# A decoder layer's opening regrouped: low parts off GpSimd, wider sums for the conditioning, four steps over K, PSUM tiles of two blocks

## The chip, the cores and the metric

The kernel runs on one core of one Trainium2 chip. The metric is the device time of one execution in microseconds, the median of the runs of one kernel. Inside a core, five engines run their own instruction queues in order and wait for each other by semaphores: TensorE (matrix products; the profile calls it PE, its weight loads PEld), VectorE (DVE), ScalarE (ACT), GpSimd (POOL) and SyncE (SP, which here only issues DMAs). Matrix products write to PSUM, eight banks of 512 f32 columns; all else lives in SBUF, 128 partitions wide.

## The reference

One decoder layer with adaLN conditioning, 256 tokens, width 2048, all f32, weights of some 630 MB read once:

```python
mods = silu(c) @ w_ada + b_ada                  # 9 vectors of 2048: shift, scale, gate, three times
sh1, sc1, g1, sh2, sc2, g2, sh3, sc3, g3 = split(mods, 9)
f1 = swiglu(x * (1 + sc1) + sh1, w_ffn1)        # 2048 -> 2 x 5632 -> 2048
x = layer_norm(alpha * x + 0.5 * g1 * f1)
m = hybrid_mixer(x * (1 + sc2) + sh2, ...)      # gated linear attention, dilated attention, output product
x = layer_norm(alpha * x + g2 * m)
f2 = swiglu(x * (1 + sc3) + sh3, w_ffn2)
x = layer_norm(alpha * x + 0.5 * g3 * f2)
```

The change concerns the start: the shift and scale of the first sub-layer are needed before any product of the first SwiGLU can be made, and they need 33.5 MB of `w_ada`.

## The kernel before

**The weight stream.** All large products run as one stream of *units*. A unit is two k-tiles (2 x 128 rows) of 512 columns of a weight, multiplied with both blocks of 128 tokens. Each f32 operand is split into two parts in a reduced format, `wh` (rounded) and `wl` (the rest), and a product is made of three matmuls (L239 to L241: high x high, high x low, low x high), so a unit is 12 matmuls. Weights come in loads of 1 MB (`raw`, an item, two units), three under way. ScalarE makes `wh` by a rounding copy (L223), VectorE or GpSimd makes `wl` by a subtraction of 128 x 1024 (L233). Who makes it is the flag `u.ve`: GpSimd for 38 units among the first 96 (units 0 and 1, then 3, 5, ... 29, then every third from 32 to 95) and for the first ones after each of the first two norms (`EARLY`, 12 units together), VectorE for all others.

**The order.** Instructions are emitted by one Python loop over units `p`, and each engine works off its queue in that order. For each `p` the loop splits unit `p + 3` (its `wh` and `wl`), emits the 12 matmuls of unit `p`, advances the side work by one step (`fl.step()`: transposes, modulation, the handling of finished sums, the norms), and then takes as many steps of the conditioning as a table `pace` of (unit, steps) demands by `p`.

**The conditioning.** `silu(c) @ w_ada` is summed on VectorE: one step (L388 the first, L390 the others) multiplies a k-tile of 512 columns by a value per partition and adds it to `part`; sixteen steps end a *piece*. Then TensorE transposes the four tiles of `part` (L424), VectorE reduces them (L341) and adds the bias (L346, L348). The first pieces, whose loads are called `abig`, hold shift and scale of the first sub-layer: two pieces with 256 columns of each, then three pairs of pieces with 512 columns of the scale and 512 of the shift. Eight pieces of 16 steps, 128 steps, precede the other seven vectors (loads called `araw`).

**The first chunks.** A *chunk* is 512 output columns. Since the modulated input becomes ready by columns, the first six gate and six up chunks are summed over K in five steps: `PHASES = ((0, 2), (2, 2), (4, 4), (8, 4), (12, 4))`, as (first k-tile, k-tiles). In steps 0 and 1 a chunk has one unit (units 0 to 11, 12 to 23), in the others two (24 to 47, 48 to 71, 72 to 95). After each step the sums leave PSUM: ScalarE copies them to `part8` after step 0, VectorE adds to it after steps 1 to 3 (L604, one 128 x 512 add for each token block), and after step 4 it adds them up and finishes the chunk (L610 to L616). `x1_groups` makes the modulated input for each group of columns (L432, L430, L410, L414).

**PSUM.** Four banks serve the sums (one tile for each token block, two chunks under way), four the transposes and other small things.

**The norms.** Behind each of the first two sub-layers, per token block: statistics (L446, L451), root and reciprocal (L458 to L460), normalising (L470), transposes, modulation, split (L408 to L432). The units of the next chunk are split during that.

```python
        while ns < min(len(units), p + 1 + SA + u.more):
            split(units[ns])
            ns += 1
        ...
        emit(u)
        fl.step()
        while ada["n"] < due(p):
            ada_step()
```

Of the kernel before, what the change touches and what calls it, by code (L numbers as in the profile page):

```python
# [35 lines left out]
# columns of the constants  # L36
# [27 lines left out]
EARLY = 10  # L64
# [7 lines left out]
class Flow:  # L72
    """Side work beside the weight stream: generators that yield where an engine has to wait for another."""
# [47 lines left out]
class Lhs:  # L121
    """An activation with features on partitions, in tiles of four k-tiles: two exact parts."""
# [12 lines left out]
class Item:  # L135
    """1 MB of a weight: G k-tiles of NC5 columns, or wide: H k-tiles of 2 * NC5"""
# [5 lines left out]
class Unit:  # L142
    def __init__(self, item, j, ts, chunk, first, last):
        self.item, self.j, self.ts, self.chunk, self.first, self.last = item, j, ts, chunk, first, last
        self.ve = self.more = 0
# [3 lines left out]
def layer(ctx, tc, a):  # L149
# [7 lines left out]
    pa = pool("pacc", 4, space=bass.MemoryType.PSUM)  # L157
# [19 lines left out]
    items, units, starts = [], [], {}  # L177

    class Chunk:
        """ps[t] = lhs[k0:k0+nk].T @ w[r0:r0+nk*P, c0:c0+512]; then done(t, ps[t])"""  # L180

        def __init__(self, w, r0, c0, nk, lhs, done, k0=0, head=False, tail=False, wide=None):
            self.lhs, self.done, self.k0, self.ps = lhs, done, k0, None
# [7 lines left out]
            seq, early = [], 0  # L191
            both = tuple(range(NT))
            n = len(its)
            gs = list(range(n))
            if head:
                seq += [(g, j, (t,)) for t in both for g in gs[:2] for j in range(2)]
                gs = gs[2:]
                early = EARLY
            mid = gs[:-2] if tail else gs
            seq += [(g, j, both) for g in mid for j in range(2)]  # L200
            if tail:
                seq += [(g, j, (t,)) for t in both for g in gs[-2:] for j in range(2)]
            for g, j, ts in seq:
                u = Unit(its[g], j, ts, self, g == 0 and j == 0, g == n - 1 and j == 1)
                u.k = k0 + g * G + j * H
                u.ve = early > 0
                early -= 1
                if early == EARLY - 1 and len(units):
                    units[-1].more = 1
                units.append(u)  # L210
# [32 lines left out]
    def emit(u):  # L243
        c, it = u.chunk, u.item
        if c.ps is None:
            fl.until(lambda: n_acc.n >= NT)
            n_acc.n -= NT
            c.ps = [pa.tile([P, NC5], F32, tag="acc", name="acc") for _ in range(NT)]
        wh, wl = it.wh[u.j]
        lhs = {(i, t): c.lhs.get(u.k + i, t) for t in u.ts for i in range(H)}  # L250
        for t in u.ts:
            for i in range(H):
                xh, xl = lhs[i, t]
                mm3(c.ps[t], xh, xl, wh[:, i], wl[:, i], u.first and i == 0, u.last and i == H - 1)
        if u.last:
            for t in u.ts:
                fl.spawn(c.done(t, c.ps[t]))

# [52 lines left out]
    def ada_load():  # L311
# [6 lines left out]
        if i < BIG:  # L318
            t = blk([P, n, NC5], name="abig")
        else:  # L320
            t = st.tile([P, n, NC5], F32, tag="araw", name="araw", bufs=3)
# [3 lines left out]
        else:  # L325
            for j in range(2):
                nc.sync.dma_start(t[:, :, j * 256:(j + 1) * 256],
                                  w[:, j * D + k0 * P:j * D + k0 * P + 256].rearrange("(k p) n -> p k n", p=P))
# [3 lines left out]
    def ada_reduce(ms, k0, nk, part, wait):  # L332
        if wait:
            yield wait
        if ms[0] in modc:
            ps = yield from mps([P, 4, P])
            transpose4(ps, part, 0)
            if ms[0] > 1:
                yield
            tot = tp.tile([P, 4], F32, tag="tot", name="tot")  # L340
            V.tensor_reduce(tot, ps, axis=mybir.AxisListType.X, op=ALU.add)  # L341
            for i, m in enumerate(ms):
                b = bcol(m)[:, k0:k0 + nk]
                o = modc[m][:, k0:k0 + nk]
                if m in PLUS1:
                    V.scalar_tensor_tensor(o, tot[:, i * nk:(i + 1) * nk], 1.0, b, op0=ALU.add, op1=ALU.add)  # L346
                else:
                    V.tensor_add(o, tot[:, i * nk:(i + 1) * nk], b)  # L348
# [19 lines left out]
    def ada_run():  # L368
        def prep(i):
# [3 lines left out]
            part = sp.tile([P, NC5], F32, tag="part", name="part", bufs=2)  # L373
# [66 lines left out]
    class Norm:  # L440
# [13 lines left out]
        def rstd(self, mv):  # L454
            """1 / sqrt(var + eps), -mean / sqrt(var + eps)"""
# [7 lines left out]
        def apply(self, t, mv, rs, nm):  # L463
            """y -> (y - mean) * rstd"""
# [9 lines left out]
    def ln_to(i, X, scm, shm, after):  # L474
        """per token block: the normalised rows, then the modulated transpose into X; then x = n * g + b"""
# [67 lines left out]
    def sqrt_ready():  # L543
        """a first square root, for its table to be there when the norm comes"""
# [22 lines left out]
    def ffn(w_gu, w_dn, X, gm, ln, norm, parts, pieced):  # L567
# [26 lines left out]
        def pieced_sink(c, e, q, sg, hT, kg):  # L594
            def done(t, ps):
                if q == 0 and (c, e, t) == (c, 0, 0):
                    partial[c] = blk([P, 2, NT, NC5], name="part8")
                p = partial[c][:, e, t]
                if q == 0:
                    A_.copy(p, ps)  # L600
                    n_acc.give()
                    return
                if q < len(PHASES) - 1:
                    V.tensor_add(p, p, ps)  # L604
                    n_acc.give()
                    return
# [11 lines left out]
            return done  # L618
# [51 lines left out]
        for pi, part in enumerate(parts):  # L670
            hT = Lhs(fl)
            if pi == 0 and pieced:
                sgs = {c: [None, None] for c in part}
                for q, (k0, nk) in enumerate(PHASES):
                    if nk == 2:
                        for c in part[::2]:
                            for e in range(2):
                                it = Item(w_gu, k0 * P, e * DFF + c * NC5, True)
                                items.append(it)
                                for i in range(2):  # L680
                                    Chunk(w_gu, 0, 0, 2, X, pieced_sink(c + i, e, q, sgs[c + i], hT, c + i),
                                          k0=k0, wide=(it, i))
                    else:
                        for c in part:
                            for e in range(2):
                                Chunk(w_gu, k0 * P, e * DFF + c * NC5, nk, X,
                                      pieced_sink(c, e, q, sgs[c], hT, c), k0=k0)
# [9 lines left out]
    # ==== sub-layer 1 ====  # L697
# [52 lines left out]
    for u in units[:2] + units[3:30:2] + units[32:96:3]:  # L750
        u.ve = 1

    # ==== sub-layer 2 ====
# [7 lines left out]
    # rope tables  # L761
# [115 lines left out]
    def tok_T(src, t, ready, dst):  # L877
        """[tok, 512] in PSUM -> dst(kpair, t, psum [P, 2, P]), features on partitions"""
# [68 lines left out]
    def head_task(h):  # L947
# [14 lines left out]
        # (output columns, partitions, keys, queries)  # L962
# [107 lines left out]
    # -- dilated attention: one softmax over the three groups' keys --  # L1070
# [130 lines left out]
    # -- gated branch b, merge --  # L1201
# [60 lines left out]
    # ==== sub-layer 3 ====  # L1262
# [9 lines left out]
    def ln3(norm, t):  # L1272
# [22 lines left out]
        for q in LN3_GP[t]:  # L1295
# [45 lines left out]
    for p, u in enumerate(units):  # L1341
        while ns < min(len(units), p + 1 + SA + u.more):
            split(units[ns])
            ns += 1
        if p in (12, 28, 50):
            fl.until(lambda: n_sml.n >= NT)
            n_sml.n -= NT
            x_load((12, 28, 50).index(p) + 1)
# [31 lines left out]
```

## Time and profile before

| | |
|---|---|
| median of 3 runs | 2754.81 us (2753.57 to 2754.82) |
| profiled execution, first to last instruction | 2753.9 us |
| TensorE busy | 2662.9 us, 97% |
| VectorE busy | 1955.0 us, 71% |
| ScalarE busy | 1201.0 us, 44% |
| GpSimd busy | 170.9 us, 6% |
| read from HBM | 645.90 MB |
| chain that ended last | TensorE 86%, VectorE 10%, issue 2% |

Engines' busy times are sums over the whole span; what bounds a stage is read from that stage alone. The profiled execution is one run; its span is 0.9 us under the median of the runs.

### The profile page before, as it was taken

The page shows a single profiled execution, that of the slowest core. Times are in us where ns is not written, and L with a number is a line of the kernel's source. Part 1 is how long each engine was busy: PE and PEld are TensorE (multiplying, and loading weights), DVE is VectorE, ACT ScalarE, POOL GpSimd, SP SyncE. Part 2 cuts the span into 40 slices and gives each one's busy share as a digit, 9 for nine tenths or more (in the row PEclk, how much of TensorE's full clock was granted, in tenths as well). Part 3 has the DMA queues.
Part 4 walks back from the last instruction along what each step waited for, and adds up shares of the span by engine and source line. Part 5 has one row for each costly group of instructions (what it writes and reads, how often), then busy time and mean ns, then how long its engine had stood idle before and what let it go on. Part 6 is the DMA issues. An engine that isn't in the chain of part 4 may idle for free.

```text
span 2753.9 us, 31250 instructions
## 1 busy us (share of the span) xinstructions
PE 2662.9 (97%) x12043; PEld 2191.7 (80%) x12043; DVE 1955.0 (71%) x2386; ACT 1201.0 (44%) x1387; POOL 170.9 (6%) x121
## 2 busy tenths in 40 slices
PE   6899999999999999999999999999999999999997
PEld 4677778888887788888888888888778888888886
DVE  7999987877766787676666676667775755655556
ACT  4233444444344654444443444554354444443443
POOL 3322200000001000000000000000110000000001
PEclk9999999999999999999999999999999999999999
DMA  9777688888874676667657767667557667656653
GB/s 341 270 266 271 223 307 306 303 291 283 282 240 165 210 271 226 214 229 238 227 186 259 247 231 242 209 223 267 196 186 258 229 225 235 230 187 210 207 191 122
DMA packets 327045, 654.24 MB, mean 238 GB/s; under 512 B 13128, under 2 KB 21552, under 8 KB 325616
## 3 DMA queue, kind: packets, MB, share of 16 engines
q1 hardware_dynamic: 322352, 633.46, 67.7%
q0 software_dynamic: 4544, 18.79, 2.1%
q8 instruction: 94, 1.54, 0.2%
q14 instruction: 55, 0.45, 0.0%
HBM read 645.90 MB, written 6.29 MB: 237 GB/s over the span
## 4 chain that ended last, share of the span: by engine, by line
PE 86%; DVE 10%; issue 2%; ACT 1%; DMA 1%; POOL 0%; SPq 0%; DVEq 0%; ACTq 0%
PE acc L239 27%; PE acc L241 27%; PE acc L240 27%; DVE part L390 3%; PE mps L424 2%; DVE wl L233 2%; DVE part L604 1%; DVE lhs L414 1%; PE mps L1163 1%; PE mps L1135 1%; ACT wh L223 0%; PE mps L973 0%; DVE sg L616 0%; DVE xm L432 0%; DMA abig<-in_w_ada 0%
## 5 line engine op out<-in xcount | busy, mean ns | idle before, releaser
L233 DVE TENSOR_TENSOR wl<-raw,wh 128x1024 fp32r<-128x1024 f32 x862 | 1066.1, 1239 | 696.2 <-ACT wh L223 694.8
L223 ACT CAST wh<-raw 128x1024 fp32r<-128x1024 f32 x912 | 957.4, 1053 | 1341.5 <-PE acc L241 1281.0
L239 PE MATMUL acc<-wh,lhs 128*128 128x512 f32 x3648 | 1445.8, 396 | 21.7 <-DVE part L604 9.7
L240 PE MATMUL acc<-wl,lhs 128*128 128x512 f32 x3648 | 1428.2, 392 | 5.7 <-DVE wl L233 4.4
L241 PE MATMUL acc<-wh,lhs 128*128 128x512 f32 x3648 | 1427.6, 391 | 0.6 <-DVE lhs L414 0.6
L239 PEld LDWEIGHTS acc<-wh,lhs 128*128 128x128 f32 x3648 | 689.5, 189 | 170.4 <-issue 8.9
L240 PEld LDWEIGHTS acc<-wl,lhs 128*128 128x128 f32 x3648 | 689.8, 189 | 152.6 <-DVE wl L233 8.1
L241 PEld LDWEIGHTS acc<-wh,lhs 128*128 128x128 f32 x3648 | 688.7, 189 | 147.7 <-DVE lhs L414 2.2
L390 DVE SCALAR_TENSOR_TENSOR part<-araw,cact,part 128x512 f32<-128x512 f32 x432 | 322.6, 747 | 0.5
L233 POOL TENSOR_TENSOR wl<-raw,wh 128x1024 fp32r<-128x1024 f32 x50 | 128.1, 2565 | 480.8 <-ACT wh L223 233.6
L390 DVE SCALAR_TENSOR_TENSOR part<-abig,cact,part 128x512 f32<-128x512 f32 x119 | 127.0, 1074 | 4.1 <-DMA abig<-in_w_ada 2.1
L604 DVE TENSOR_TENSOR part<-part,acc 128x512 f32<-128x512 f32 x72 | 46.1, 679 | 1.8 <-PE acc L241 1.8
L376 POOL DMA_DIRECT2D part<-in_b_ada x12 | 6.1, 506 | 627.3 <-DVE part L375 186.9
L414 DVE TENSOR_TENSOR lhs<-mps,lhs 128x512 fp32r<-128x512 f32 x64 | 41.3, 683 | 1.6 <-ACT lhs L410 1.6
L410 ACT CAST lhs<-mps 128x512 fp32r<-128x512 f32 x64 | 34.5, 586 | 0.0
L1064 POOL DMA_DIRECT2D mgd<-sga x8 | 4.3, 541 | 458.6 <-DVE sga L1062 457.8
L424 PE MATMUL mps<-ident,part 128*128 128x128 f32 x96 | 16.6, 300 | 15.6 <-DVE part L390 15.1
L414 DVE TENSOR_TENSOR lhs<-xm,lhs 128x256 fp32r<-128x256 f32 (+1 forms) x34 | 23.7, 714 | 10.3 <-ACT lhs L410 9.7
L424 PEld LDWEIGHTS mps<-ident,part 128*128 128x128 f32 x96 | 12.5, 153 | 20.4 <-DVE part L390 17.6
L1138 DVE TENSOR_TENSOR sS<-mps,consts 128x128 f32<-128x128 f32 (+1 forms) x48 | 16.0, 358 | 14.9 <-PE mps L1135 14.5
L612 ACT ACTIVATE sg<-sg 128x512 f32<-128x512 f32 x12 | 7.4, 633 | 43.9 <-DVE sg L610 43.9
L578 ACT ACTIVATE sg<-acc 128x512 f32<-128x512 f32 x32 | 19.0, 598 | 16.0 <-PE acc L241 16.0
(222 smaller groups left out, 942.2 us busy)
## 6 DMA issues: line engine op xcount, KB each, us to landing
raw<-in_w_ffn_gu SPq DMA_DIRECT2D x176, 1024.0 KB, 5.0
raw<-in_w_in SPq DMA_DIRECT2D x152, 1024.0 KB, 5.0
araw<-in_w_ada SPq DMA_DIRECT2D x224, 512.0 KB, 5.5
raw<-in_w_ffn_down SPq DMA_DIRECT2D x88, 1024.0 KB, 5.0
abig<-in_w_ada SPq DMA_DIRECT2D x24, 1024.0 KB, 7.9
raw<-in_w_branch_a SPq DMA_DIRECT2D x16, 1024.0 KB, 5.5
raw<-in_w_out SPq DMA_DIRECT2D x16, 1024.0 KB, 6.6
raw<-in_w_branch_b SPq DMA_DIRECT2D x8, 1024.0 KB, 4.9
```

What stands on the lines that cost most here:

```text
L223: A_.copy(wh, r)
L233: (nc.gpsimd if u.ve else V).tensor_sub(wl, r, wh.bitcast(F32))
L239: T.matmul(ps, lhsT=xh, rhs=wh, start=first, stop=False)
L240: T.matmul(ps, lhsT=xh, rhs=wl, start=False, stop=False)
L241: T.matmul(ps, lhsT=xl, rhs=wh, start=False, stop=last)
L390: V.scalar_tensor_tensor(pt, w, cact[:, k:k + 1], pt, op0=ALU.mult, op1=ALU.add)
L410: A_.copy(hs, src)
L414: V.tensor_sub(b[:, 1, j, t * P:(t + 1) * P], src, b[:, 0, j, t * P:(t + 1) * P].bitcast(F32))
L424: T.transpose(ps[:, j], src[:, c0 + j * P:c0 + (j + 1) * P], ident)
L604: V.tensor_add(p, p, ps)
L1135: T.matmul(ps[:, 0:nk], lhsT=qk[g][:, 0, j, t * P:(t + 1) * P], rhs=qk[g][:, 1, j, 0:nk], start=True, stop=True)
L1163: T.matmul(ops[:, 0:HD], lhsT=pTs[kb][:, g], rhs=d["v"][g][:, kb, j * HD:(j + 1) * HD], start=i == 0, stop=i == n_mm - 1)
```

## The change

Five edits belong together. No low part is made on GpSimd any more, neither in the opening nor after the norms, and the extra split ahead (`more`) goes. The conditioning's three pairs of pieces become three pieces of 1024 columns, scale and shift side by side, each step 128 x 1024; their 1 MB loads become two DMAs of half that size with half as many k-tiles, and `part` takes a buffer of the `araw` loads. The first vectors take 80 steps, not 128. The first chunks are summed in four steps of K, the last over eight k-tiles, four units a chunk (units 48 to 95). Both token blocks of a chunk share one PSUM tile of two banks, and after the first three steps one instruction handles both. The pace follows.

```diff
+SUMS = ((0, 2), (2, 2), (4, 4), (8, 8))
...
-        (nc.gpsimd if u.ve else V).tensor_sub(wl, r, wh.bitcast(F32))
+        V.tensor_sub(wl, r, wh.bitcast(F32))
...
-    pa = pool("pacc", 4, space=bass.MemoryType.PSUM)
+    pa = pool("pacc", 2, space=bass.MemoryType.PSUM)
...
-            c.ps = [pa.tile([P, NC5], F32, tag="acc", name="acc") for _ in range(NT)]
+            c.pair = pa.tile([P, NT, NC5], F32, tag="acc", name="acc")
+            c.ps = [c.pair[:, t] for t in range(NT)]
...
-        if u.last:
+        if u.last and c.both:
+            fl.spawn(c.done(c.pair))
+        elif u.last:
...
-        pieces += [((0, 1), k0, 2, 4 if k0 else 2)] if nk == 2 else [((1,), k0, 4, 4), ((0,), k0, 4, 4)]
+        pieces.append(((0, 1), k0, nk, 2 if nk == 4 or not k0 else 4))
...
-            t = blk([P, n, NC5], name="abig")
+            t = blk([P, n, len(ms) * nk * P], name="abig")
...
+            if len(pieces[i][0]) * pieces[i][2] == 8:
+                part = st.tile([P, 2 * NC5], F32, tag="araw", name="part", bufs=3)
...
+            def add(pair):
+                if (q, e) == (0, 0):
+                    partial[c] = blk([P, 2, NT, NC5], name="part8")
+                p = partial[c][:, e]
+                if q == 0:
+                    A_.copy(p, pair)
+                else:
+                    V.tensor_add(p, p, pair)
+                n_acc.give(NT)
...
-                for q, (k0, nk) in enumerate(PHASES):
+                for q, (k0, nk) in enumerate(SUMS):
...
-    for u in units[:2] + units[3:30:2] + units[32:96:3]:
-        u.ve = 1
...
-    pace = [(-1, 16), (5, 32), (20, 64), (42, 96), (66, 128), (n1 - 20, 320), (n1 + 8, 320), (n3 - 20, 512),
-            (n3 + 8, 512), (len(units) - 110, 576), (len(units) + 1, 576)]
+    pace = [(-1, 16), (5, 32), (20, 48), (33, 64), (45, 80), (n1 - 20, 272), (n1 + 8, 272), (n3 - 20, 464),
+            (n3 + 8, 464), (len(units) - 110, 528), (len(units) + 1, 528)]
...
-        while ns < min(len(units), p + 1 + SA + u.more):
+        while ns < min(len(units), p + 1 + SA):
...
-        if p in (12, 28, 50):
+        if p in (12, 24, 36):
```

## Rows read from the trace of the kernel before

**Rows 1.** The page's first line.
```profile
span 2753.9 us, 31250 instructions
```

**Rows 2.** Windows, all engines: stretch and length, busy us (instructions), clock, DMA share, GB/s.
```profile
24.50:51.60 27.10, 21.59 (x88) 17.26 (x87) 25.57 (x21) 16.43 (x23) 13.72 (x5) 0.97 1.06 404
51.60:121.30 69.70, 56.80 (x224) 44.39 (x224) 65.51 (x79) 22.67 (x31) 21.42 (x8) 0.89 0.78 281
121.30:198.90 77.60, 72.94 (x305) 58.30 (x305) 70.59 (x84) 30.81 (x37) 20.95 (x9) 0.93 0.74 267
...
276.90:356.20 79.30, 73.02 (x331) 57.76 (x330) 75.00 (x85) 32.23 (x43) 19.83 (x10) 1.00 0.70 239
356.20:800.00 443.80, 442.81 (x1990) 366.43 (x1990) 346.26 (x406) 190.29 (x202) 7.04 (x12) 1.00 0.86 294
```

**Rows 3.** Windows, L240 alone: PE busy (matmuls), PEld busy, clock, DMA share, GB/s.
```profile
0.00:121.30 121.30, 40.99 (x96) 20.29 (x96) 0.93 0.87 320
0.00:205.40 205.40, 83.27 (x200) 40.76 (x201) 0.93 0.80 292
0.00:276.90 276.90, 118.32 (x288) 57.84 (x289) 0.94 0.79 285
0.00:356.20 356.20, 156.20 (x384) 75.86 (x384) 0.95 0.77 275
356.20:800.00 443.80, 246.96 (x634) 119.19 (x635) 1.00 0.86 294
```

**Rows 4.** Chain of waits, 30 to 60 us: start, us, what.
```profile
33.96 2.78 DVE part L390
```

**Rows 5.** Timeline of GpSimd, 33 to 34 us: start, us, instruction, idle before.
```profile
33.67 2.51 POOL L233 TENSOR_TENSOR wl<-raw,wh 128x1024 fp32r<-128x1024 f32 x1 [3.40 <-ACT wh L223]
```

**Rows 6.** VectorE by line, 24.5 to 51.6 us: busy us, mean ns, idle before.
```profile
L390 DVE SCALAR_TENSOR_TENSOR part<-abig,cact,part 128x512 f32<-128x512 f32 x15 | 17.4, 1161 | 0.4
L233 DVE TENSOR_TENSOR wl<-raw,wh 128x1024 fp32r<-128x1024 f32 x4 | 6.2, 1554 | 0.9 <-ACT wh L223 0.9
L388 DVE TENSOR_SCALAR part<-abig,cact 128x512 f32<-128x512 f32 x1 | 2.4, 2412 | 0.1
```

**Rows 7.** VectorE by line, 51.6 to 124.1 us.
```profile
L390 DVE SCALAR_TENSOR_TENSOR part<-abig,cact,part 128x512 f32<-128x512 f32 x32 | 34.2, 1068 | 0.7
L233 DVE TENSOR_TENSOR wl<-raw,wh 128x1024 fp32r<-128x1024 f32 x8 | 14.1, 1768 | 0.0
L604 DVE TENSOR_TENSOR part<-part,acc 128x512 f32<-128x512 f32 x22 | 14.0, 679 | 0.0
```

**Rows 8.** VectorE by line, 124.1 to 198.9 us.
```profile
L390 DVE SCALAR_TENSOR_TENSOR part<-abig,cact,part 128x512 f32<-128x512 f32 x31 | 31.7, 1023 | 0.5
L233 DVE TENSOR_TENSOR wl<-raw,wh 128x1024 fp32r<-128x1024 f32 x15 | 20.4, 1363 | 0.0
L604 DVE TENSOR_TENSOR part<-part,acc 128x512 f32<-128x512 f32 x24 | 15.5, 679 | 1.8 <-PE acc L241 1.8
```

**Rows 9.** VectorE by line, 357 to 800 us.
```profile
L233 DVE TENSOR_TENSOR wl<-raw,wh 128x1024 fp32r<-128x1024 f32 x160 | 195.8, 1224 | 96.2 <-ACT wh L223 95.9
L390 DVE SCALAR_TENSOR_TENSOR part<-araw,cact,part 128x512 f32<-128x512 f32 x156 | 116.1, 744 | 0.3
```

**Rows 10.** Chain of waits, 822 to 845 us, the first norm.
```profile
823.48 1.94 DVE nm L460
825.43 5.06 DVE f L470 x2
```

**Rows 11.** Timeline of VectorE, 839 to 841 us, the same norm's second block.
```profile
839.91 0.16 DVE L460 SCALAR_TENSOR_TENSOR nm<-mv,rs 128x1 f32<-128x1 f32 x1
839.99 1.00 DVE L470 TENSOR_SCALAR f<-f,mv,rs 128x512 f32<-128x512 f32 x2
```

**Rows 12.** L233 on VectorE, 24 to 357 us: what it waited for (us, times).
```profile
  ACT wh L223: 4.6, 6
```

**Rows 13.** Timeline of VectorE, 822 to 860 us: three low parts in a row.
```profile
855.40 3.49 DVE L233 TENSOR_TENSOR wl<-raw,wh 128x1024 fp32r<-128x1024 f32 x3
```

More of the change, by code (lines that the diff above doesn't have):

```diff
@@ L59 @@
 PHASES = ((0, 2), (2, 2), (4, 4), (8, 4), (12, 4))
+SUMS = ((0, 2), (2, 2), (4, 4), (8, 8))
 ADA0 = 8
 ADA_FLIGHT = 3
-EARLY = 10
 LN_STEPS = ((3, 1, 1, 5), (2, 2, 0, 3))
@@ L144, in __init__ @@
         self.item, self.j, self.ts, self.chunk, self.first, self.last = item, j, ts, chunk, first, last
-        self.ve = self.more = 0
 @with_exitstack
@@ L179, in layer, with __init__ @@
     class Chunk:
-        def __init__(self, w, r0, c0, nk, lhs, done, k0=0, head=False, tail=False, wide=None):
-            self.lhs, self.done, self.k0, self.ps = lhs, done, k0, None
+        def __init__(self, w, r0, c0, nk, lhs, done, k0=0, head=False, tail=False, wide=None, both=False):
+            self.lhs, self.done, self.k0, self.ps, self.both = lhs, done, k0, None, both
             if wide:
@@ L190, in __init__ @@
             items.extend(its)
-            seq, early = [], 0
+            seq = []
             both = tuple(range(NT))
@@ L197, in __init__ @@
                 gs = gs[2:]
-                early = EARLY
             mid = gs[:-2] if tail else gs
@@ L205, in __init__ @@
                 u.k = k0 + g * G + j * H
[L206 to L209, printed above, removed]
                 units.append(u)
@@ L326, in ada_load @@
             for j in range(2):
-                nc.sync.dma_start(t[:, :, j * 256:(j + 1) * 256],
-                                  w[:, j * D + k0 * P:j * D + k0 * P + 256].rearrange("(k p) n -> p k n", p=P))
+                n2 = nk * P
+                nc.sync.dma_start(t[:, :, j * n2:(j + 1) * n2],
+                                  w[:, j * D + k0 * P:j * D + k0 * P + n2].rearrange("(k p) n -> p k n", p=P))
         ada["tiles"][i, g0] = t
@@ L335, in ada_reduce @@
         if ms[0] in modc:
-            ps = yield from mps([P, 4, P])
-            transpose4(ps, part, 0)
+            groups = [(ms, 0)] if len(ms) * nk == 4 else [((m,), i * NC5) for i, m in enumerate(ms)]
+            pss = []
+            for _, c0 in groups:
+                ps = yield from mps([P, 4, P])
+                transpose4(ps, part, c0)
+                pss.append(ps)
             if ms[0] > 1:
                 yield
[L340 to L348, printed above, removed]
+            for (gm, _), ps in zip(groups, pss):
+                tot = tp.tile([P, 4], F32, tag="tot", name="tot")
+                V.tensor_reduce(tot, ps, axis=mybir.AxisListType.X, op=ALU.add)
+                for i, m in enumerate(gm):
+                    b = bcol(m)[:, k0:k0 + nk]
+                    o = modc[m][:, k0:k0 + nk]
+                    if m in PLUS1:
+                        V.scalar_tensor_tensor(o, tot[:, i * nk:(i + 1) * nk], 1.0, b, op0=ALU.add, op1=ALU.add)
+                    else:
+                        V.tensor_add(o, tot[:, i * nk:(i + 1) * nk], b)
+            n_mps.give(len(groups) - 1)
         else:
@@ L372, in prep @@
             (m, *_), k0 = pieces[i][:2]
-            part = sp.tile([P, NC5], F32, tag="part", name="part", bufs=2)
+            if len(pieces[i][0]) * pieces[i][2] == 8:
+                part = st.tile([P, 2 * NC5], F32, tag="araw", name="part", bufs=3)
+            else:
+                part = sp.tile([P, NC5], F32, tag="part", name="part", bufs=2)
             if m not in modc:
@@ L594, in pieced_sink @@
         def pieced_sink(c, e, q, sg, hT, kg):
+            def add(pair):
[4 more added lines that the diff above has]
+                    A_.copy(p, pair)
+                else:
+                    V.tensor_add(p, p, pair)
+                n_acc.give(NT)
+                return
+                yield
             def done(t, ps):
-                if q == 0 and (c, e, t) == (c, 0, 0):
-                    partial[c] = blk([P, 2, NT, NC5], name="part8")
                 p = partial[c][:, e, t]
[L599 to L606, printed above, removed]
                 if e == 0:
@@ L617, in done @@
                     yield from up_tail(t, sg, hT, kg)
-            return done
+            return add if q < len(SUMS) - 1 else done
         def fold():
@@ L673, in ffn @@
                 sgs = {c: [None, None] for c in part}
-                for q, (k0, nk) in enumerate(PHASES):
+                for q, (k0, nk) in enumerate(SUMS):
+                    both = q < len(SUMS) - 1
                     if nk == 2:
@@ L681, in ffn @@
                                     Chunk(w_gu, 0, 0, 2, X, pieced_sink(c + i, e, q, sgs[c + i], hT, c + i),
-                                          k0=k0, wide=(it, i))
+                                          k0=k0, wide=(it, i), both=both)
                     else:
@@ L686, in ffn @@
                                 Chunk(w_gu, k0 * P, e * DFF + c * NC5, nk, X,
-                                      pieced_sink(c, e, q, sgs[c], hT, c), k0=k0)
+                                      pieced_sink(c, e, q, sgs[c], hT, c), k0=k0, both=both)
             else:
@@ L1341, in layer @@
     for p, u in enumerate(units):
-        while ns < min(len(units), p + 1 + SA + u.more):
+        while ns < min(len(units), p + 1 + SA):
             split(units[ns])
             ns += 1
-        if p in (12, 28, 50):
+        if p in (12, 24, 36):
             fl.until(lambda: n_sml.n >= NT)
             n_sml.n -= NT
-            x_load((12, 28, 50).index(p) + 1)
+            x_load((12, 24, 36).index(p) + 1)
         for gen in starts.get(p, ()):
```

## The prediction

> **What bounds the kernel now.** I read the windows by stage first, then the by-line tables of VectorE in the same stretches, then the chain of waits and the timeline in three short windows. The span is 2753.9 us [rows 1]; the median of the runs shown, 2754.81, is 0.9 us above it, which I add at the end. Four matmuls of L240 make one unit of the weight stream, so a count of them dates the units: unit 24 starts at 121.3 us, unit 50 at 205.4, unit 72 at 276.9, unit 96 at 356.2 [rows 3]. From 356.2 to 800 TensorE is 99.8% busy [rows 2] and passes 634 of these, 158.5 units, in 443.8 us: 2.80 us a unit with its side work [rows 3]. At that pace 96 units from 24.5 us on would end at 293; they end at 356.2, so the opening loses 63 us. In its stages shown VectorE is 91 to 95% busy, TensorE 80 to 94% [rows 2]: VectorE bounds the opening. From 356 to 800 it doesn't (78%). Of the rest only the two norms are touched, where the chain runs over VectorE too.
>
> **Where VectorE's time goes.** One step of the conditioning (L390) takes 0.744 us in a stretch without GpSimd low parts [rows 9]. The step at 33.96 takes 2.78 and ends 0.6 us after GpSimd's low part, which began at 33.67 and took 2.51 [rows 4, 5]. I read the excess as VectorE held up by GpSimd. By stage, taking off the means of 357 to 800 (0.744 for L390, 1.224 for L233): 24.5 to 51.6 has 15 x 0.417 + 4 x 0.330 + 1.7 for L388 (2.41 less a step) = 9.3 us [rows 6]; 51.6 to 124.1 has 32 x 0.324 + 8 x 0.544 = 14.7 [rows 7]; 124.1 to 198.9 has 31 x 0.279 + 15 x 0.139 = 10.7 [rows 8].
>
> **Prices.** A low part on VectorE: three in a row take 3.49 us, 1.16 each [rows 13]. A 1024-wide step isn't in the trace. A 512-wide add is 0.679 [rows 7], a 1024-wide difference 1.224 [rows 9], so another 512 columns cost 0.54, and 0.744 + 0.54 = 1.28 us. Bounds: 1.22 (that 1024-wide difference) and 1.49 (two narrow steps). I take 1.28, as both its terms are VectorE's own. A pair add: 0.679 + 0.54 = 1.22; bounds 1.36 (no better than two adds) and 1.08 (twice 0.54). I take 1.20.
>
> **The first 51.6 us.** Unit 0's low part now stands in VectorE's queue ahead of the first two modulated tiles: 1.16 us there against GpSimd's 2.5, both ahead of the second matmul; I count it as even. Then the second piece, not widened, sets the end: its 16th step releases the transposes that TensorE waits for. The stage loses 9.3 us of hold-ups and gains the low parts of units 1, 3, 5 and 7, 4 x 1.16 = 4.6. It ends 4.7 us earlier, at 46.9.
>
> **To unit 24.** Hold-ups -14.7; nine low parts (odd units 9 to 25) +10.4; 35 narrow steps (26.0) become 18 wide ones (23.0), -3.0; 11 pairs of adds, 11 x (1.36 - 1.20) = -1.8. Sum -9.1: unit 24 starts at 121.3 - 4.7 - 9.1 = 107.5, and all the features that it needs are there at 124.1 - 13.8 = 110.3.
>
> **Units 24 to 50.** Here the change costs. Before, the sums' fourth step took k-tiles 8 to 11 (from unit 48) and the fifth 12 to 15 (from unit 72); now the fourth takes 8 to 15, so unit 50 needs the last columns, and the new pace has the last wide step at unit 45 where the old one had the last narrow one at 66. From 110.3 VectorE must do 23 low parts (units 26 to 48), 26.7; 30 wide steps, 38.4; 13 pair adds, 15.6; and one group's reductions, modulation and waits, which is what is left of the same group before: 74.8 - 31.7 - 20.4 - 15.5 = 7.2 us [rows 8]. Sum 87.9: the last step ends at 198.2. TensorE then has eight transposes and units 47 to 49 to do, about 9.4 us, and VectorE brings the last columns in about that time; unit 50 starts at 207.6, 2 us later than before. All that is won to unit 24 is paid back here.
>
> **Units 50 to 96.** The gain shows here: the third add of the partial sums is gone, the wide steps are done, and nothing holds VectorE up. For eight units (a gate and an up chunk) VectorE has 8 x 1.16 = 9.3 of low parts, 8 x 0.946 x 0.744 = 5.6 of steps at the new pace, eight operations of some 0.68 to finish the chunks, 5.4, and 0.5 for gates: 20.8 us against TensorE's 22.4 at 2.80. So TensorE should bound. Its side work (two groups of four transposes in eight units) is denser here than from 356 to 800; I take 2.88 us a unit, near the lower of the bounds 2.80 and 3.30 (the last 24 units before, 79.3 us). 46 x 2.88 = 132.5, so unit 96 starts at 340.1 against 356.2: -16.1. From there both kernels have the same units. The pace is lighter on VectorE (192 steps over 203 units, not 182), but TensorE was at 99.8% there: worth nothing.
>
> **The two norms.** In the first, on the chain, a 128x1 product takes 1.94 us where its like takes 0.16, and two normalising steps 5.06 where two take 1.00 [rows 10, 11]: 5.8 us of hold-up by GpSimd low parts. These go to VectorE; by the order of the main loop one stands ahead of the reciprocal and one between the normalised rows and the modulation, 1.2 to 2.3 us on the path. Net -3.5 to -4.6; the later low parts and the lost extra split ahead are about even. I take -4 for each norm, -8. That the second is like the first is assumed from the same code.
>
> **At nothing.** Twelve pair copies on ScalarE replace 24: ScalarE is 33 to 61% busy in the opening [rows 2]; without that cover they'd cost some 12 x 1 us. The pair in PSUM frees both blocks at once where one could go first: a chunk two places on waits for it, at most half an add, 0.6 us, for each of 24 chunks, but VectorE's own queue is longer than that. Low parts wait in VectorE's queue for ScalarE's rounding copy, which GpSimd did on its own: those already on VectorE waited 4.6 us in 59 [rows 12], so 38 more might wait 3.
>
> **Sum.** 2753.9 - 16.1 - 8 + 0.9 = **2731 us**.
>
> **The queue of loads.** From 24.5 to 51.6 it is full and moves 404 GB/s; later 239 to 281, with 22 to 30% of its time free [rows 2]. Loads of 1 MB become two of half that, 24 more issues on SP's queue; the second piece's loads are split so already and lie in the 404 stretch, so I count nothing. The Trainium skill, "DMA: Bandwidth & Descriptors", section "Rules for kernel authors", speaks against this edit: it asks for 1 MiB or more in each DMA. By that rule the queue would be slower and rival (c) nearer; the 404 GB/s don't bear it out.
>
> **Rivals.**
> (a) VectorE still bounds to unit 96. Either the wide step costs 1.49, +0.21 x 46 = 9.7 us by unit 50, or TensorE keeps half of today's loss after it, (3.30 - 2.88) / 2 x 46 = 9.7. For it: 20.8 of 22.4 us is tight, in one in-order queue. Against it: the hold-ups that make today's loss are gone. 2741; with the norms' gain lost too, 2749.
> (b) The gain isn't there: the long rows are waits that come back under other names. If half of the 46 us (34.7 to unit 48, 11.6 in the norms) come back, the time is today's, 2755. Against it: 156 steps without GpSimd beside them have a mean of 0.744 [rows 9].
> (c) Slower: the queue of loads becomes the bound. Until unit 50 it must bring 33.6 MB of the conditioning (before 25.2), 26.2 of weights, 2 of x and some 3 ahead, 65 MB. At 404 GB/s that is 161 us, at 275, the mean from 0 to 356.2 [rows 3], 236: unit 50 would start 28 us late, the time 2759. It decides from 65 / (208 + 24) = 280 GB/s downwards. For it: after 51.6 no stage of the opening shows more than 281. Against it: they leave a quarter of the queue's time unused.
>
> **How the numbers follow.** Forecast 0.62 (its own range 2720 to 2738), (a) 0.20, (b) 0.07, (c) 0.08, and 0.03 that the time is under 2714, with VectorE no bound from early on. Two in ten lie outside from 2714 to 2747: (a) is inside but for its end, (b) and (c) are out. A change within 0.2%, 5.5 us, can hardly be told from none. Faster 0.85, same 0.07, slower 0.08.
>
> **What would show it.** No narrow L390 row over 1.4 us and wide ones of 1.25 to 1.35; no GpSimd low part; 200 matmuls of L240 by 203 to 212 us, 384 by 336 to 345; TensorE over 97% busy between; the norm's 128x1 product at 0.16. I am wrong if unit 50 comes after 215 (step price or queue), or if TensorE waits for low parts after it.

## The result, and the profile after

The kernel after takes 2726.32 us (median of 4 runs, 2724.76 to 2726.88); the kernel before, run beside it, 2754.19. The ratio is 0.9899, with an interval from 0.9885 to 0.9913: faster by 28 us. The forecast was 2731, in a range from 2714 to 2747.

The first two lines of the new page (the first answers [rows 1]; the second has each engine's busy time, its share of the span and its instructions):

```profile
span 2724.4 us, 31105 instructions
...
PE 2650.9 (97%) x12043; PEld 2186.4 (80%) x12043; DVE 1901.3 (70%) x2340; ACT 1196.4 (44%) x1375; POOL 42.8 (2%) x71
```

The matmuls of the second product alone, which is now L233 (windows, with the columns of [rows 3]). The counts are the same 96, 200, 288 and 384, so the ends of these windows are the starts of units 24, 50, 72 and 96:

```profile
0.00:106.00 106.00, 37.96 (x96) 18.48 (x96) 1.00 0.98 364
0.00:203.20 203.20, 81.22 (x200) 39.73 (x201) 0.96 0.89 329
0.00:265.30 265.30, 115.52 (x288) 56.27 (x288) 0.97 0.87 316
0.00:333.80 333.80, 152.92 (x384) 74.33 (x384) 0.97 0.85 309
```

Unit 24 starts 15.3 us earlier than before, unit 50 only 2.2, unit 72 11.6, unit 96 22.4. What was won to unit 24 is given back by unit 50 and won anew behind it. All engines by those stages (windows, columns of [rows 2]):

```profile
23.50:46.90 23.40, 21.67 (x93) 17.58 (x93) 21.76 (x27) 17.73 (x21) 0.00 (x0) 1.00 1.06 401
46.90:106.00 59.10, 50.72 (x223) 39.17 (x221) 57.05 (x62) 22.32 (x26) 0.00 (x0) 0.99 0.97 362
106.00:203.20 97.20, 84.06 (x345) 66.68 (x346) 89.32 (x92) 32.98 (x43) 0.51 (x1) 0.92 0.79 291
203.20:265.30 62.10, 62.10 (x283) 51.62 (x282) 55.05 (x68) 30.81 (x36) 0.48 (x1) 1.00 0.80 273
265.30:333.80 68.50, 68.50 (x315) 56.97 (x315) 60.16 (x75) 32.24 (x38) 2.08 (x4) 1.00 0.80 280
```

VectorE (the third pair of numbers) is 92 to 97% busy up to unit 50. Behind it TensorE (the first pair) is busy for the whole of both windows: there VectorE bounds nothing any more. VectorE's rows by line from 46.9 to 203.2 us, which answer to [rows 7, 8]:

```profile
L396 DVE SCALAR_TENSOR_TENSOR part<-abig,cact,part 128x1024 f32<-128x1024 f32 x45 | 57.4, 1276 | 0.3
L226 DVE TENSOR_TENSOR wl<-raw,wh 128x1024 fp32r<-128x1024 f32 x42 | 51.1, 1217 | 0.0
L608 DVE TENSOR_TENSOR part<-part,acc 128x1024 f32<-128x1024 f32 x24 | 29.1, 1213 | 1.9 <-PE acc L234 1.9
```

The wide step takes 1.276 us (1.28 was taken), the pair add 1.213 (1.20). No row is long: the longest wide step takes 1.29 us, the longest narrow one 0.75, and the excess of [rows 6 to 8] is gone. VectorE in the first norm (timeline), which answers to [rows 10, 11]:

```profile
799.41 1.23 DVE L226 TENSOR_TENSOR wl<-raw,wh 128x1024 fp32r<-128x1024 f32 x1 [1.10 <-ACT wh L216]
800.56 0.16 DVE L465 RECIPROCAL rs<-rs 128x1 f32<-128x1 f32 x1
800.75 0.16 DVE L466 SCALAR_TENSOR_TENSOR nm<-mv,rs 128x1 f32<-128x1 f32 x1
800.82 1.91 DVE L476 TENSOR_SCALAR f<-f,mv,rs 128x512 f32<-128x512 f32 x4
802.65 1.22 DVE L226 TENSOR_TENSOR wl<-raw,wh 128x1024 fp32r<-128x1024 f32 x1
```

The product that took 1.94 us takes 0.16, and the two low parts stand where they were expected, one ahead of the reciprocal and one behind the normalised rows.

### The profile page after: what moved, and what is told of

Its sections match the earlier page's. It is cut to its first block, busy times and chain, and to the rows that moved or that the text cites. A ratio compares the mean times of both kernels' runs of the same rounds, so it can differ in the third digit from the quotient of the medians.

```text
span 2724.4 us, 31105 instructions
## 1 busy us (share of the span) xinstructions
PE 2650.9 (97%) x12043; PEld 2186.4 (80%) x12043; DVE 1901.3 (70%) x2340; ACT 1196.4 (44%) x1375; POOL 42.8 (2%) x71
## 4 chain that ended last, share of the span: by engine, by line
PE 89%; DVE 6%; DMA 1%; issue 1%; ACT 1%; SPq 0%; DVEq 0%
PE acc L234 28%; PE acc L232 28%; PE acc L233 28%; PE mps L430 2%; DVE part L396 2%; DVE wl L226 1%; DMA abig<-in_w_ada 1%; DVE part L608 1%; PE mps L1169 1%; PE mps L1141 1%; PE mps L979 0%; ACT wh L216 0%; DVE xm L438 0%; PE mps L1158 0%; DMA raw<-in_w_ffn_gu 0%
## 5 line engine op out<-in xcount | busy, mean ns | idle before, releaser
L226 DVE TENSOR_TENSOR wl<-raw,wh 128x1024 fp32r<-128x1024 f32 x912 | 1112.6, 1223 | 695.5 <-ACT wh L216 693.6
L233 PE MATMUL acc<-wl,lhs 128*128 128x512 f32 x3648 | 1426.3, 391 | 4.6 <-DVE wl L226 4.6
L233 PEld LDWEIGHTS acc<-wl,lhs 128*128 128x128 f32 x3648 | 688.4, 189 | 147.6 <-DVE wl L226 7.4
L396 DVE SCALAR_TENSOR_TENSOR part<-abig,cact,part 128x1024 f32<-128x1024 f32 (+1 forms) x74 | 78.4, 1070 | 2.2 <-DMA abig<-in_w_ada 1.5
L608 DVE TENSOR_TENSOR part<-part,acc 128x1024 f32<-128x1024 f32 x24 | 29.1, 1213 | 1.9 <-PE acc L234 1.9
L584 ACT ACTIVATE sg<-acc 128x512 f32<-128x512 f32 x32 | 17.4, 596 | 25.8 <-PE acc L234 25.8
L416 ACT CAST lhs<-xm 128x512 fp32r<-128x512 f32 (+1 forms) x18 | 10.3, 573 | 36.8 <-DVE xm L438 36.4
L595 DVE TENSOR_TENSOR sg<-sg,acc 128x512 f32<-128x512 f32 x32 | 20.6, 684 | 6.5 <-PE acc L234 6.5
L420 DVE TENSOR_TENSOR lhs<-xm,lhs 128x256 fp32r<-128x256 f32 (+1 forms) x34 | 17.6, 531 | 9.2 <-ACT lhs L416 8.5
L430 PEld LDWEIGHTS mps<-ident,sg 128*128 128x128 f32 x176 | 20.5, 140 | 2.8
L430 PE MATMUL mps<-ident,sg 128*128 128x128 f32 x176 | 22.8, 272 | 0.0
```

The costliest lines, as they stand in the source:

```text
L226: V.tensor_sub(wl, r, wh.bitcast(F32))
L233: T.matmul(ps, lhsT=xh, rhs=wl, start=False, stop=False)
L396: V.scalar_tensor_tensor(pt, w, cact[:, k:k + 1], pt, op0=ALU.mult, op1=ALU.add)
L416: A_.copy(hs, src)
L420: V.tensor_sub(b[:, 1, j, t * P:(t + 1) * P], src, b[:, 0, j, t * P:(t + 1) * P].bitcast(F32))
L430: T.transpose(ps[:, j], src[:, c0 + j * P:c0 + (j + 1) * P], ident)
```

## The experiments

Ten kernels ran. The times are medians; the kernel before, run beside them, took 2754.11 in the first group of four, 2754.19 in the second and 2753.40 with the last two, so the times can be set side by side. The starts of units are counted in each trace as above (12 matmuls a unit). "Four sums" and "five sums" are the four steps of K of the change and the five of the kernel before:

| kernel | us | ratio (95%) | unit 24 | 50 | 72 | 96 |
|---|---|---|---|---|---|---|
| before | 2754.2 | | 121.3 | 205.4 | 276.9 | 356.2 |
| after | 2726.32 | 0.9899 (0.9885 to 0.9913) | 106.0 | 203.2 | 265.3 | 333.8 |
| before, low parts on VectorE | 2718.43 | 0.987 (0.9855 to 0.9885) | 110.3 | 187.5 | 252.2 | 328.2 |
| after, opening's low parts on GpSimd | 2747.77 | 0.9975 (0.9965 to 0.9985) | 115.9 | 218.9 | 285.5 | 356.5 |
| after, norms' low parts on GpSimd | 2735.27 | 0.9933 (0.9917 to 0.995) | 106.1 | 203.1 | 265.2 | 333.7 |
| after, single PSUM tiles | 2722.53 | 0.9886 (0.9872 to 0.9901) | 107.1 | 204.1 | 266.2 | 334.6 |
| after, five sums | 2713.57 | 0.9854 (0.9837 to 0.987) | 104.7 | 179.2 | 241.8 | 317.7 |
| five sums, single PSUM tiles | 2710.32 | 0.984 (0.9825 to 0.9855) | 105.5 | 180.1 | 243.4 | 319.3 |
| the same, lighter pace | 2701.49 | 0.9809 (0.9794 to 0.9824) | 105.6 | 181.1 | 243.1 | 312.8 |
| before, low parts on VectorE, four sums | 2735.78 | 0.9933 (0.9918 to 0.9948) | 110.9 | 216.8 | 278.9 | 347.4 |
| after, GpSimd reads beside | 2759.81 | 1.0021 (1.0012 to 1.003) | 119.4 | 238.1 | 300.2 | 368.7 |
| after, GpSimd writes beside | 2725.60 | 0.9898 (0.9882 to 0.9915) | 106.4 | 203.2 | 265.3 | 333.8 |

**One part alone: only the low parts moved.** The kernel before with

```diff
-        (nc.gpsimd if u.ve else V).tensor_sub(wl, r, wh.bitcast(F32))
+        V.tensor_sub(wl, r, wh.bitcast(F32))
...
-        while ns < min(len(units), p + 1 + SA + u.more):
+        while ns < min(len(units), p + 1 + SA):
```

> The kernel before with one part of the change alone: every low part on VectorE, no extra split ahead; steps, sums and PSUM tiles as before. My theory (GpSimd holds VectorE up for longer than a low part costs it): the three stages to 199 us give 34.7 us of hold-ups and take 22 low parts, 25.5, the two stages after it give 28 and take 16, 18.6, so unit 96 comes 12 to 18 us earlier; the norms give some 6. 2730 to 2737. Rival (the regrouping of steps and sums carries the gain, the low parts cost the same on either engine): 2750 to 2756, and unit 96 within 3 us of 356.

2718.43: 7.9 us *less* than the whole change, and below the range expected. The five edits together are worth less than this one. Two of its stages (windows, all engines; 24 to 50 and 72 to 96 by units):

```profile
110.30:187.50 77.20, 75.15 (x329) 61.13 (x329) 73.32 (x99) 32.48 (x38) 0.00 (x0) 0.98 0.82 294
...
252.20:328.20 76.00, 72.18 (x330) 58.32 (x331) 71.81 (x95) 31.98 (x43) 0.97 (x2) 1.00 0.73 239
```

It passes units 24 to 50 in 77.2 us where the kernel after takes 97.2, and units 72 to 96 in 76.0 where that one takes 68.5. So the other four edits cost 20.0 us in the one place and win 7.5 in the other, and they win 4.3 before unit 24 and 2.6 from 50 to 72: 5.6 us lost by unit 96.

**Two parts undone: GpSimd back in the opening, GpSimd back at the norms.** Each puts the flags of the kernel before back on the kernel after, for one of the two places, and at the norms the extra split ahead as well:

```diff
+        (nc.gpsimd if u.ve else V).tensor_sub(wl, r, wh.bitcast(F32))
...
+    for u in units[:2] + units[3:30:2] + units[32:96:3]:
+        u.ve = 1
```

> The changed kernel with the 38 low parts of the opening back on GpSimd; all else as changed. My theory: 22 low parts leave VectorE by unit 48, -25.5 us, and hold it up for some 22 x 1.8 = 40; from unit 50 to 96, where VectorE has about 10% of its time free, half of 16 x (1.8 - 1.16) shows. 2738 to 2748. Rival (placement is neutral, regrouping is the gain): 2723 to 2729.

```diff
+                early = 10
...
+                u.ve = early > 0
...
+        while ns < min(len(units), p + 1 + SA + u.more):
```

> The changed kernel with the first low parts behind the first two norms back on GpSimd, and the extra split ahead with them. My theory: each norm gives back the 3.6 and 3.8 us that unit starts show it gained, 2731 to 2736, and the 128x1 product of the norm takes 1.9 us again. Rival (the norms' gain comes from another place, such as the lighter pace): 2725 to 2728.

Both times lie in their ranges: the opening's low parts are worth 2747.77 - 2726.32 = 21.5 us, the norms' 2735.27 - 2726.32 = 9.0. In the second the 128x1 product of the norm takes 2.05 us again, and the normalising step behind it, which reads one tile and two values for each partition, 2.65 us where four take 1.91 without GpSimd: an instruction with a single tile for its input can be held up too. In the first the wide steps have a mean of 1.647 us (lines, 24 to 357 us), while the pair adds stay at 1.212:

```profile
L397 DVE SCALAR_TENSOR_TENSOR part<-abig,cact,part 128x1024 f32<-128x1024 f32 x45 | 74.1, 1647 | 0.5
...
L609 DVE TENSOR_TENSOR part<-part,acc 128x1024 f32<-128x1024 f32 x24 | 29.1, 1212 | 3.4 <-PE acc L235 3.3
```

**One part undone: a PSUM tile for each block.**

```diff
-    pa = pool("pacc", 2, space=bass.MemoryType.PSUM)
+    pa = pool("pacc", 4, space=bass.MemoryType.PSUM)
...
-            c.pair = pa.tile([P, NT, NC5], F32, tag="acc", name="acc")
-            c.ps = [c.pair[:, t] for t in range(NT)]
+            c.ps = [pa.tile([P, NC5], F32, tag="acc", name="acc") for _ in range(NT)]
...
```

> The changed kernel with one PSUM tile for each token block; what one instruction did for the pair is done by two. My theory: 24 adds of the pair become 48 of half the width, 24 x 0.15 = 3.6 us more on VectorE, almost all before unit 50; against it the tails of the norms no longer wait 0.95 us for the first block's sums, which the norm's own chain hides. 2727 to 2731. Rival (the shared tile costs more in waits than it saves: 0.95 us in two tails and 0.5 in four other places show it in the unit starts): 2722 to 2725.

The rival was right: 2722.53, 3.8 us less. The shared tile and its pair adds win 0.8 us by unit 96 and lose it behind: against single tiles the kernel after stands 0.8 ahead at unit 96, 0.3 behind at unit 270, 2.3 behind at 640 and 3.8 behind at 900. How far two traces of nearly the same program lie apart can be seen from the run with the writing GpSimd: from unit 50 on each unit starts within 0.7 us of the kernel after's. One place is the tail of the last chunk ahead of the first norm. The timeline of TensorE in the kernel after, at the change from the first block's matmuls to the second's:

```profile
795.45 0.39 PE L234 MATMUL acc<-wh,lhs 128*128 128x512 f32 x1
796.62 0.51 PE L232 MATMUL acc<-wh,lhs 128*128 128x512 f32 x1 [0.78 <-DVE res L669]
```

The second block's matmul waits until VectorE has read the first block's sums (L669, 795.87 to 796.56), which lie in the other bank of the same tile. With single tiles no such wait is listed; the second norm's tail shows it too, 0.8 us. Over each of the two tails the kernel after loses 1.1 us by its unit starts. Another 2.0 are lost between units 270 and 640, where two waits of the mixer's small products are longer than with single tiles, 1.1 us against 0.3 and 1.0 against 0.4. That the tile costs these 2.0 us follows from the two runs; why those waits are longer, and what the rest of the loss consists of, stays open.

**The regrouping undone: five sums on the kernel after.** The low parts, the wide steps and the shared tile stay:

```diff
-SUMS = ((0, 2), (2, 2), (4, 4), (8, 8))
+SUMS = PHASES
...
-    pace = [(-1, 16), (5, 32), (20, 48), (33, 64), (45, 80), ...
+    pace = [(-1, 16), (5, 32), (20, 48), (42, 64), (66, 80), ...
...
-        if p in (12, 24, 36):
+        if p in (12, 28, 50):
```

> The kernel after with the five steps of K of the kernel before (the last columns needed from unit 72 on, not 50), and the conditioning's steps spread over as many units as before; the wide steps and the shared PSUM tile stay. Theory A (the regrouping into four steps pulls VectorE's work in front of unit 50 and so costs what the earlier run without it won): unit 50 starts near 187 us (after: 203.2), unit 96 near 325 (after: 333.8), time 2716 to 2720. Theory B (what the kernel after lacks against the one that only moves the low parts lies in the wide steps and their split loads): unit 50 stays at 200 or later, unit 96 at 332 to 336, time 2724 to 2729.

2713.57, 12.8 us under the kernel after and better than theory A asked. Its stage from unit 24 to 50 (windows):

```profile
104.70:179.20 74.50, 73.86 (x329) 59.95 (x330) 70.92 (x70) 32.62 (x38) 0.00 (x0) 1.00 0.84 308
```

TensorE is 99% busy at a granted clock of 1.00, where the kernel after has 86% at 0.92. The stage takes 74.5 us, not 97.2.

**The regrouping alone, on narrow steps.** The second kernel of this list with `SUMS` and the pace of the change:

```diff
+SUMS = ((0, 2), (2, 2), (4, 4), (8, 8))
...
-    pace = [(-1, 16), (5, 32), (20, 64), (42, 96), (66, 128), ...
+    pace = [(-1, 16), (5, 32), (20, 64), (33, 96), (45, 128), ...
...
```

> The kernel before with the low parts on VectorE and the four steps of K and the earlier pace of the change, but with the narrow 512-column pieces and one PSUM tile for each block. Theory A (the regrouping alone is what costs): unit 50 near 212 us (with the low parts alone: 187.5), unit 96 near 340 (328.2), time 2728 to 2733, against 2718.4 with the low parts alone. Theory B (the wide steps and loads are what costs): unit 50 under 195, time 2716 to 2721.

2735.78, 17.4 us slower than without the regrouping (2718.43), a little over theory A's range: unit 50 starts 29.3 us later and unit 96 still 19.2. Its stage from unit 24 to 50:

```profile
110.90:216.80 105.90, 85.06 (x345) 66.45 (x346) 97.69 (x136) 33.71 (x43) 0.51 (x1) 0.90 0.77 278
```

Here VectorE has 97.7 us of work in the stage where it had 73.3 without the regrouping, and the wait of TensorE that costs most in it (us in total, times, longest) is for the steps that end the conditioning's pieces; without the regrouping that wait is 0.5 us in the same stage:

```profile
PE mps L425 <- DVE part L391: 17.1, 4, 5.2
```

**Wide steps without the regrouping, and a lighter pace.** Five sums with single PSUM tiles (the edit above), and the same with one more entry in the pace, which puts off the other vectors' steps from units 80 to 96:

> The same with one PSUM tile for each token block again: of the change, only the low parts on VectorE and the wide steps are left. Theory A, with the shared tile costing the 3.8 us measured: 2712 to 2717, some 3 to 4 under the run with the shared tile, and 1 to 6 under the run that has only the low parts moved (2718.4), since 45 wide steps replace 90 narrow ones at 1.276 against 2 x 0.749, 10 us less on VectorE. Theory B: 2720 to 2725, slower than with the low parts alone.

```diff
-    pace = [(-1, 16), (5, 32), (20, 48), (42, 64), (66, 80), (n1 - 20, 272), ...
+    pace = [(-1, 16), (5, 32), (20, 48), (42, 64), (66, 80), (96, 84), (n1 - 20, 272), ...
```

> The same again, but with the steps of the seven other vectors put off from units 80 to 96 to after unit 96 (4 instead of some 17 there), where TensorE has been the bound. If VectorE bounds to unit 96, some 13 steps of 0.74 us fewer ahead of it: unit 96 6 to 10 us earlier than without, time 2704 to 2710. If TensorE already bounds from unit 72 on, no difference: within 2 us of the run without.

The first takes 2710.32, 8.1 us under the low parts alone and a little more than expected: that is what the wide steps and their loads of half the size are worth together. The second takes 2701.49, 8.8 us less again, a little beyond its range too, and the fastest of all, 52.7 us under the kernel before. Its last stage, units 72 to 96:

```profile
243.10:312.80 69.70, 69.70 (x329) 58.16 (x328) 58.93 (x73) 36.90 (x46) 0.00 (x0) 1.00 0.65 206
```

TensorE is busy throughout; with the pace as it was, the same stage took 75.9 us.

**The hold-up by itself.** On the kernel after, beside VectorE's own low part of 18 units (13, 15, ... 47), GpSimd either makes the same difference into a buffer that nobody reads, or copies one column and fills that buffer twice:

```diff
+        if u in beside:
+            nc.gpsimd.tensor_sub(scr, r, wh.bitcast(F32))
...
+    beside += units[13:48:2]
```

> The kernel after, and beside VectorE's low part of 18 units (13, 15, ... 47) GpSimd makes the same difference once more, into a buffer that nobody reads: VectorE has no instruction less or more. Theory H (VectorE's instructions with two SBUF inputs are held up while GpSimd reads SBUF): wide steps and low parts that lie beside it get long; the earlier run with 21 low parts of the opening on GpSimd started unit 50 15.7 us later although VectorE had some 25 us less to do, about 41 / 21 = 1.9 us for each; so 18 x 1.6 to 1.9 us, unit 50 at 232 to 238 (after: 203.2), time 2750 to 2760; the mean of a wide step rises from 1.276 to 1.6 or more, the pair adds, which have an input in PSUM, stay at 1.21. Rival L (what costs is that the weight's buffer comes free later, since GpSimd must have read it too): the means stay at 1.28 and 1.22, VectorE waits instead, and the time is under 2735.

```diff
+        if u in beside:
+            nc.gpsimd.tensor_copy(scr[:, 0, 0:1], wh[:, 0, 0:1].bitcast(F32))
+            for _ in range(2):
+                nc.gpsimd.memset(scr, 0.0)
```

> The kernel after, and beside the same 18 low parts GpSimd copies one column of the high part and then fills 1024 columns of the unread buffer twice, so that it is busy about as often but reads next to nothing. Theory H (it is GpSimd's reading that holds VectorE up): unit 50 within 2 us of 203.2, means 1.28 and 1.22, time 2725 to 2730. Rival W (any GpSimd access to SBUF holds VectorE up): the wide step's mean rises over 1.45 and the time over 2738.

Theory H holds in both, at the upper end of its range in the first. With the reading GpSimd the time is 2759.81, slower than the kernel before, and unit 50 starts 34.9 us late. VectorE and GpSimd by line, 47 to 235 us:

```profile
L399 DVE SCALAR_TENSOR_TENSOR part<-abig,cact,part 128x1024 f32<-128x1024 f32 x45 | 75.1, 1669 | 0.3
L227 DVE TENSOR_TENSOR wl<-raw,wh 128x1024 fp32r<-128x1024 f32 x42 | 68.4, 1628 | 0.0
L611 DVE TENSOR_TENSOR part<-part,acc 128x1024 f32<-128x1024 f32 x24 | 29.0, 1208 | 1.0 <-PE acc L237 1.0
...
L230 POOL TENSOR_TENSOR consts<-raw,wh 128x1024 f32<-128x1024 f32 x18 | 52.5, 2919 | 143.8 <-ACT wh L217 133.0 <-issue 10.0 <-POOL consts L230 0.8
```

The same 45 steps and 42 low parts take 45 x 0.393 + 42 x 0.411 = 35.0 us more, 1.94 for each of GpSimd's 18 differences, and that is the whole delay; the pair adds, one of whose inputs lies in PSUM, are as they were, and VectorE doesn't wait more. The writing GpSimd leaves the same rows alone:

```profile
L227 DVE TENSOR_TENSOR wl<-raw,wh 128x1024 fp32r<-128x1024 f32 x54 | 65.7, 1217 | 1.0 <-ACT wh L217 1.0
L401 DVE SCALAR_TENSOR_TENSOR part<-abig,cact,part 128x1024 f32<-128x1024 f32 x45 | 57.4, 1276 | 0.3
...
L232 POOL MEMSET consts<- 128x1024 f32 x36 | 34.4, 956 | 2.1
```

Units 50 to 264 start within 0.1 us of the kernel after's, with GpSimd busy for 54 us in the opening. The one-column copies do read SBUF, but next to nothing: the 16 steps and low parts that begin beside one of them take their usual 1.22 to 1.29 us, as do the 11 that begin beside a fill. The Trainium skill, "SBUF — State Buffer", section "Who interferes with whom", says the same: a VectorE instruction with two SBUF inputs contends with a GpSimd instruction that reads SBUF, "not with one that only writes it". These two runs agree with it, at 1.94 us for each reading instruction of a whole tile and none for the writing ones.

## Why the prediction was right, point by point

**The hold-up.** That the long rows of VectorE come from GpSimd was read from one step and one low part [rows 4, 5] and is now shown by adding and taking away. Rival (b), that they would come back under other names, is out.

**To unit 24.** 107.5 was worked out, 106.0 measured; the transposes that end the first stage start at 46.5 (51.6 before), where 46.9 was worked out.

**Units 24 to 50.** 207.6 was worked out, 203.2 measured. Two terms of it were off, with opposite signs. From the features at hand to the last wide step there were 87.9 us in the sum; they were at hand at 108.7, and the step ends at 191.3, 82.6 us later. The chain of waits at that point:

```profile
188.92 1.13 DVE part L608
190.05 1.21 DVE part L396
191.26 0.04 issue
191.30 1.97 PE mps L430 x8
193.27 0.43 PE acc L232
...
199.96 0.23 PE acc L232
```

An add that has a row of 1.213 us and a step with one of 1.276 hold the chain for 1.13 and 1.21: the next instruction starts before the row of the one ahead ends. The sum had low parts by their distance (1.16) but steps and adds by their rows; 0.07 to 0.08 for each of 43 is some 3 us of the 5.3 by which it was too long. The rest is smaller: 12 of the 13 adds come before the last step (1.2 us), the first step of the piece takes 0.75 us and not 1.28 (0.5), and low parts follow each other after 1.13 to 1.14 us and not 1.16 (0.6). The other term, eight transposes and three units, was 9.4 us and took 11.9, since TensorE came out of a pause at half its clock (below).

That this stage pays back what unit 24 had won was right; but the prediction put it down as the price of the change as it is, and never asked what the change would be without it. It had no term for that, so its range says nothing of it; the runs show the price: the regrouping with its pace costs 17.4 us on narrow steps and 12.8 on wide ones. It moves the last columns' need from unit 72 to unit 50, into the stretch where VectorE bounds, and wins back only 10.1 us (narrow) or 7.9 (wide) by a smooth run from unit 50 to 96, and 1.6 to 2.0 more by unit 260.

**Units 50 to 96.** 2.88 us a unit was taken, 130.6 / 46 = 2.84 measured, with no TensorE wait listed from 203 to 334 us. Rival (a) is out for this kernel, though not for its neighbours: with five sums and the old pace, VectorE bounds units 72 to 96 again (75.9 us), until the lighter pace takes its steps away (69.7). The prediction's remark on the pace as worth nothing spoke of the stretch behind unit 96, and there it was 2 us off: the seven kernels with four sums go from unit 96 to 260 in 456.4 us, the five with five sums in 457.4 to 458.6. Of the 2.2 us between before and after, 1.7 come by unit 102, where TensorE in the kernel before still waits 1.0 us for low parts and in the kernel after for none; whether the pace or the sums' order brings them was not taken apart.

**The norms.** -8 was taken. Putting GpSimd back there alone costs 9.0; in the kernel after the norms bring 3.2 + 3.8 = 7.0 against before, since the shared tile's two tails of 1.1 us stand against it.

**At nothing.** The shared PSUM tile is the step that failed: it was weighed against VectorE's queue in the opening, where it does cost nothing, and not in the tails ahead of the norms, where one block's sums are read while the other block's are still to be made (1.1 us each), nor in the mixer (2.0, by waits whose cause is not shown). In all it costs 3.8 us. The three others held: ScalarE's pair copies (1.01 us each; TensorE waits for one of the twelve, 0.4 us), the low parts' waits for the rounding copy (6.7 us ahead of L226 from 24.5 to 357, where 4.6 were seen and 3 more allowed for) and the queue of loads.

**The queue of loads, rival (c).** 329 GB/s to unit 50 [after's windows of L233], above the 280 from which it would decide; from 106 to 203 us VectorE's listed waits are 4.8 us for ScalarE and 1.9 for TensorE, none for a load. The chain of waits does name two loads there, 5.33 us from 103.31 and 8.19 from 166.59, but VectorE works on beside both: from 108.6 to 191.3 it is never idle for more than 0.06 us but for 2.1 us ahead of two splits that wait for ScalarE. The first stage moves 401 GB/s, and ten of the fourteen loads issued in it have half a megabyte.

**The sum.** Set against the trace before, unit 260 starts 24.6 us earlier (16.1 was taken to unit 96; 22.4 came, and 2.2 more behind it), the first norm adds 3.2, 2.0 are lost up to unit 640, and 3.8 come between 640 and 900; the end is 29.5 us earlier. The profiled run lies 1.9 us under its median, where 0.9 was added. Part of the nearness of 2731 to 2726 is luck: the opening came out 8.5 us better than its term, against which stand 1.0 at the norms, 2.0 in the mixer that the sum did not have, and 1.0 in what lies between a profiled run and the median.

## What to carry to other kernels

Time a bundle of edits part by part even when the bundle wins: here one edit of five was worth 35.7 us alone, and the bundle 28. When side work sits ahead of a stream, ask which unit needs its last result: here a regrouping that moved that unit forward cost more than the instructions it saved. A buffer shared by two users has to be followed to every place where one is read while the other is written, not only where the change was meant to act.

## What the runs showed of the hardware

**A held-up instruction ends a set time after GpSimd's.** From the run with the reading GpSimd, its timeline and VectorE's:

```profile
59.03 2.63 POOL L230 TENSOR_TENSOR consts<-raw,wh 128x1024 f32<-128x1024 f32 x1 [54.10 <-ACT wh L217]
64.10 3.24 POOL L230 TENSOR_TENSOR consts<-raw,wh 128x1024 f32<-128x1024 f32 x1 [2.44 <-ACT wh L217]
```

```profile
59.31 3.43 DVE L399 SCALAR_TENSOR_TENSOR part<-abig,cact,part 128x1024 f32<-128x1024 f32 x1
...
63.80 1.27 DVE L399 SCALAR_TENSOR_TENSOR part<-abig,cact,part 128x1024 f32<-128x1024 f32 x1
65.00 3.42 DVE L227 TENSOR_TENSOR wl<-raw,wh 128x1024 fp32r<-128x1024 f32 x1
```

GpSimd's instructions end at 61.66 and 67.34, VectorE's that began inside them at 62.74 and 68.42: 1.08 us later both times, a little less than they take alone. The step at 63.80, which began ahead of GpSimd's second, has its usual 1.27. In all 18 of that run's GpSimd differences the held-up wide step or low part ends 1.08 or 1.09 us after GpSimd's; a narrow step in the kernel before ends 0.56 us after it (33.96 + 2.78 against 33.67 + 2.51 in [rows 4, 5]). GpSimd is held up likewise: 14 of the 18 begin while a step or a low part of VectorE runs and end 2.20 to 2.27 us after that one, in rows of 2.5 to 3.3 us; the three that begin beside none take 2.34 to 2.41.

**A pause of TensorE costs twice.** The end of the regrouped stage in the kernel after (windows of TensorE alone: busy us, clock, DMA share, GB/s):

```profile
188.00:192.00 4.00, 0.70 (x4) 0.80 0.66 247
192.00:196.00 4.00, 4.00 (x13) 0.50 0.40 109
196.00:200.00 4.00, 4.00 (x16) 0.85 0.74 284
```

TensorE is busy for 0.70 of 4 us while VectorE ends the last columns, a loss by itself, and comes back at a granted clock of 0.50, the level of 1.2 GHz; in the chain above a matmul then holds 0.43 us, not 0.23. Unit 47 takes 4.81 us, units 48 and 49 2.74 and 2.72. With five sums there is no such pause between units 24 and 50, and the clock stays at 1.00.
